# A 64-byte spacer at the right end of SBUF in a one-core decoder-layer kernel

## Chip, core and metric

The kernel runs on one core of one Trainium2 chip. The metric is the device time of one execution in microseconds (us). The core has five engines with queues of their own: TensorE (PE, matmuls, with its weight loads listed as PEld), VectorE (DVE), ScalarE (ACT), GpSimd (POOL) and SyncE (SP, which here only starts DMAs). The on-chip memory SBUF has 128 partitions; a tile takes the same range of bytes in each partition, and "begins at byte b" below means that range.

## The reference

One layer of a hybrid decoder, batch 1, 1024 tokens, width 1024, all in float32:

```
hn = rmsnorm(x);  proj = hn @ w_in          # 3592 columns
attention: 4 heads, two softmaxes each, ALiBi, out = (p0 - lam * p1) @ v
mLSTM:     4 heads, causal conv + silu on q and k, chunked matrix memory
x  = x + concat(da_out, ml_out) @ w_out
hn = rmsnorm(x)
u  = causal_dwconv(hn @ w_up, width 3)      # 2 x 2816 columns
x  = x + (silu(gate) * up) @ w_down
out = rmsnorm(x)
```

## The kernel before

Every large float32 product is made of three PE matmuls on operands that were split into a high and a low part (`split`, L109: ACT writes the high part, DVE or POOL the rest; both lie in one tile `[P, 2, 512]`). `mm3` (L154) issues them as L155, L156 and L157: high times high, high times low, low times high; `mm3b` (L159, lines L160 to L162) does the same in another order. In the rows of the profile the operand behind `<-` that is named first is the **moving** one, which is streamed through the array in 512 columns, and the second the **stationary** one, which is loaded beforehand: `mm<-xb,w` streams `xb` against weights from `w`. Where both come from tiles of one name, the row has the name once (`big<-w`).

The program goes through these stages on the one PE:

1. Input projection and gates (0 to about 215 us): `xb` (the split input) and `w` (split weights), moving and stationary in either role. The gate columns `wg16` (L408) are a small stationary operand of their own.
2. mLSTM chunks (to about 300 us) with the last projections as filler.
3. Attention (to about 500 us), with projections of the next head and of the output as filler; scores are L746 (`ks` against `qs`) and L747 (`kl` against `qz`).
4. Output projection (to about 571 us): stationary `mxT` (L792), moving `w` and then `th`.
5. Up-projection (about 571 to 1004 us): `product` (L1010) runs 154 times, 7 for each of 22 column blocks (a Strassen scheme of 7 products on halves), and issues 12 `mm3` matmuls each time, 1848 in all. Stationary is `w`, written by `prep` (L971), which is kept LEAD = 5 products ahead; moving are the blocks of the activations in `hb`, `th`, `raw`, `B22h`, `B22l` and, for the low parts of some, `x2a`.
6. Down-projection (about 1004 to 1211 us): `dmm` with both operands in tiles `w`, `w2` and the like, then the final norm.

All instructions of an engine stand in the order in which the code issues them; waits follow from the tiles that instructions share. Tiles get their addresses from pools, which are stacks. A pool without a side grows from low bytes upward (`cp`, `sp`, `wp`, `px`, later `px2`, `pmx`, `pf`, `pd`). A pool with `side="right"` grows downward from the top (`pr0`, `pq`, `pa` at L166 to L168; `pb`, `pat`, and for stages 5 and 6 `ph0` and `phn`, which hold `hb`, `B22`, `raw` and `th`). Nearly all tiles have sizes that are multiples of 128 bytes, so all tiles of one side share their start modulo 128, apart from a few small ones and `vext` and `Cst` of the mLSTM.

Of the kernel before, what the change touches and what calls it, by code (L numbers as in the profile page):

```python
# [10 lines left out]
F32 = mybir.dt.float32  # L11
# [6 lines left out]
P = 128  # L18
# [21 lines left out]
def tile_hybrid(ctx: ExitStack, tc: tile.TileContext, I: dict, out: bass.AP):  # L40
# [10 lines left out]
    class Scope:  # L51
# [8 lines left out]

        def close(self):
            self.st.close()

    wp = Scope("wp")

# [1289 lines left out]
```

## Time and profile before

| what | us |
|---|---|
| three runs | 1217.51, 1219.83, 1223.55 (median 1219.83) |
| the profiled execution, whole time | 1226.28 |
| its span, first to last instruction | 1224.5 |
| PE busy in the span | 1196.4 (98%) |
| DVE, ACT, POOL busy | 898.4, 572.5, 476.9 |
| mean granted TensorE clock | 0.995 of full speed |

The page gives busy times of each engine, a strip of 40 slices of the span, the DMA queues, the chain of work that ended last (followed back from the last instruction) and groups of instructions by line with their mean duration. Windows count each engine's busy time and instructions in a stretch of the span; the timeline lists instructions by start. The page says of itself that matmuls are pipelined and that their ends are modelled: a matmul's listed duration overlaps the next one, so the pace of PE is read from starts, or from the number of matmuls in a window in which PE never idles.

### The profile page before, as it was taken

To read this page: it belongs to the slowest core of one execution; us is meant where nothing else is said; L and a number is where in the kernel's file an instruction comes from. 1 tells how busy PE (TensorE), PEld (TensorE's weight loads), DVE (VectorE), ACT (ScalarE), POOL (GpSimd) and SP (SyncE) were. 2 spreads that over 40 slices of the span, in tenths; PEclk is the share of its full clock that TensorE was granted. 3 is DMA by queue.
4 is the path that set the end of the run, shared out by engine and by line. 5 is a ranking of instruction groups with operands and counts; after the bars stand their busy time and mean duration, and the time that the engine had idled before them with its cause. 6 is when DMAs were issued, how large, how long until landed. Compare 5 with 4: busy or idle time off the path is not lost.

```text
span 1224.5 us, 15939 instructions
## 1 busy us (share of the span) xinstructions
PE 1196.4 (98%) x5622; PEld 976.5 (80%) x5622; DVE 898.4 (73%) x1564; ACT 572.5 (47%) x1114; POOL 476.9 (39%) x364
## 2 busy tenths in 40 slices
PE   9998999999999999999999999999999999999996
PEld 7885778888778878888888888888888888888885
DVE  5599222566767777679998978787787778896694
ACT  6533323334666664444643443434344345544462
POOL 0475451004544421001398877777777600000000
PEclk9998999999999999999999999999999999999999
DMA  8755574124222252433222221212212158832223
GB/s 301 260 209 201 212 251 154 62 80 154 80 50 56 65 178 87 144 119 113 85 71 102 90 100 69 86 69 86 88 68 103 53 212 321 307 105 95 95 78 137
DMA packets 61743, 159.03 MB, mean 130 GB/s; under 512 B 6176, under 2 KB 10464, under 8 KB 61664
## 3 DMA queue, kind: packets, MB, share of 16 engines
q1 hardware_dynamic: 61232, 157.21, 37.4%
q8 instruction: 44, 0.72, 0.2%
q10 hardware_dynamic: 432, 0.82, 0.2%
q14 instruction: 35, 0.29, 0.1%
HBM read 116.02 MB, written 37.78 MB: 126 GB/s over the span
## 4 chain that ended last, share of the span: by engine, by line
PE 82%; DVE 6%; DMA 5%; ACT 3%; POOL 3%; issue 1%; SPq 0%; POOLq 0%; DVEq 0%; ACTq 0%
PE mm L157 6%; PE mm L155 6%; PE mm L156 6%; PE big L155 5%; PE big L157 5%; PE big L156 5%; PE mm L160 4%; PE mm L161 4%; PE mm L162 4%; PE big L160 3%; PE big L161 3%; PE big L162 3%; PE sb L774 3%; PE sb L155 2%; PE sa L155 2%; PE sa L157 2%
## 5 line engine op out<-in xcount | busy, mean ns | idle before, releaser
L112 ACT ACTIVATE w<-wf 128x512 fp32r<-128x512 f32 x160 | 98.1, 625 | 139.1 <-PE mm L157 36.6
L113 DVE TENSOR_TENSOR w<-wf,w 128x512 fp32r<-128x512 f32 x128 | 106.1, 840 | 25.8 <-ACT w L112 21.6
L1038 DVE SCALAR_TENSOR_TENSOR y<-x2b,fcw,y 128x1022 f32<-128x1022 f32 x44 | 90.7, 2100 | 0.0
L1037 DVE SCALAR_TENSOR_TENSOR y<-x2b,fcw,y 128x1023 f32<-128x1023 f32 x44 | 75.1, 1745 | 10.6 <-ACT y L1036 10.6
L324 POOL TENSOR_TENSOR vda<-vda 128x512 f32<-128x512 f32 x24 | 47.9, 2011 | 62.1 <-DMA vda<-in_w_down_dram 61.3
L113 POOL TENSOR_TENSOR w<-s,w 128x512 fp32r<-128x512 f32 x40 | 68.8, 1721 | 7.1 <-ACT w L112 7.1
L113 POOL TENSOR_TENSOR w<-wf,w 128x512 fp32r<-128x512 f32 x32 | 46.2, 1446 | 58.0 <-ACT w L112 48.1
L113 POOL TENSOR_TENSOR w<-wu,w 128x512 fp32r<-128x512 f32 x40 | 66.1, 1651 | 4.0 <-ACT w L112 4.0
L155 PE MATMUL mm<-xb,w 128*128 128x512 f32 x168 | 66.2, 394 | 0.0
L157 PE MATMUL mm<-xb,w 128*128 128x512 f32 x168 | 65.9, 392 | 0.0
L156 PE MATMUL mm<-xb,w 128*128 128x512 f32 x168 | 65.9, 392 | 0.0
L749 DVE CUSTOM_DVE_ANT_0 s<-big,B 128x128 f32<-128x128 f32 (+7 forms) x64 | 47.6, 755 | 13.7 <-PE big L747 12.3
L1036 ACT ACTIVATE y<-x2b,fcw 128x1024 f32<-128x1024 f32 x44 | 52.3, 1237 | 11.1 <-DVE x2b L1027 9.7
L965 POOL TENSOR_TENSOR s<-wu 128x512 f32<-128x512 f32 x20 | 32.0, 1601 | 58.5 <-DMA wu<-in_w_up_dram 58.5
L751 ACT ACTIVATE s<-s,mb 128x128 f32<-128x128 f32 (+7 forms) x64 | 49.3, 772 | 11.2 <-DVE mb L750 10.1
L160 PE MATMUL big<-w 128*128 128x512 f32 x132 | 51.5, 390 | 0.8 <-DVE x L1199 0.8
L112 ACT ACTIVATE w<-s 128x512 fp32r<-128x512 f32 x43 | 27.0, 629 | 52.3 <-PE mm L157 18.6
L161 PE MATMUL big<-w 128*128 128x512 f32 x132 | 51.4, 389 | 0.0
L162 PE MATMUL big<-w 128*128 128x512 f32 x132 | 51.4, 389 | 0.0
L112 ACT ACTIVATE w<-wu 128x512 fp32r<-128x512 f32 x48 | 29.7, 626 | 43.7 <-PE mm L157 13.5
L1027 DVE TENSOR_TENSOR x2b<-x2b,mm 128x512 f32<-128x512 f32 x51 | 34.1, 681 | 20.4 <-PE mm L157 19.7
L1027 DVE TENSOR_TENSOR x2b<-x2b,big 128x512 f32<-128x512 f32 x53 | 35.4, 680 | 18.5 <-PE big L157 17.9
(514 smaller groups left out, 3802.5 us busy)
## 6 DMA issues: line engine op xcount, KB each, us to landing
wf<-in_w_up_dram SPq DMA_DIRECT2D x22, 512.0 KB, 4.4
actd<-y SPq DMA_DIRECT2D x21, 512.0 KB, 2.6
wu<-in_w_up_dram SPq DMA_DIRECT2D x20, 512.0 KB, 3.4
wf<-in_w_st_dram SPq DMA_DIRECT2D x12, 512.0 KB, 4.2
vda<-in_w_down_dram SPq DMA_DIRECT2D x12, 512.0 KB, 5.9
wsum<-vda SPq DMA_DIRECT2D x12, 512.0 KB, 3.1
wf<-in_w_mv_dram SPq DMA_DIRECT2D x12, 512.0 KB, 5.2
wf<-wsum SPq DMA_DIRECT2D x12, 512.0 KB, 3.4
```

Source lines behind the costliest of these rows:

```text
L112: A.activation(dst[:, 0, :], src, AF.Copy)
L113: loeng.tensor_tensor(dst[:, 1, :], src, dst[:, 0, :].bitcast(F32), op=ALU.subtract)
L155: PE.matmul(ps, sh, mh, start=first, stop=False)
L156: PE.matmul(ps, sh, ml, start=False, stop=False)
L157: PE.matmul(ps, sl, mh, start=False, stop=last)
L160: PE.matmul(ps, sh, w[:, 0, :], start=first, stop=False)
L161: PE.matmul(ps, sl, w[:, 0, :], start=False, stop=False)
L162: PE.matmul(ps, sh, w[:, 1, :], start=False, stop=last)
L1027: V.tensor_tensor(dst, src, ps, op=ALU.add)
L1036: A.activation(y, u, AF.Identity, bias=cw[:, 3:4], scale=cw[:, 2:3])
L1037: V.scalar_tensor_tensor(y[:, 1:], u[:, :S - 1], cw[:, 1:2], y[:, 1:], op0=ALU.mult, op1=ALU.add)
L1038: V.scalar_tensor_tensor(y[:, 2:], u[:, :S - 2], cw[:, 0:1], y[:, 2:], op0=ALU.mult, op1=ALU.add)
```

## The change

A pool of one tile of 16 float32 (64 bytes in each partition) is opened first on the right side. It is never written or read. Every later pool on the right side starts 64 bytes lower; nothing else in the code differs.

```diff
         def close(self):
             self.st.close()
+
+
+    ctx.enter_context(tc.tile_pool(name="pad", bufs=1, side="right")).tile([P, 16], F32, name="padr")

     wp = Scope("wp")
```

No instruction is added, removed or moved on any engine, and every wait is on the same semaphore and value. What differs is the start byte of 316 of the program's tiles, all on the right side. The two programs place the operands that PE reads most as follows (start byte modulo 128, and where the tiles of that name lie before):

| tile | side | bytes before | before, mod 128 | after, mod 128 |
|---|---|---|---|---|
| `w`, `xb`, `mxT`, `w2`, `x2a` | left | 32416 to 122528 | 32 | 32 |
| `th`, `raw` | right | 126944 to 180192 | 96 | 32 |
| `hb`, `B22h`, `B22l` | right | 180192 to 229344 | 96 | 32 |
| `ks`, `kl`, `qs`, `qz`, `s`, `aT`, `vda`, `mqk`, `ta` | right | 131040 to 221152 | 96 | 32 |
| `wg16` | right | 149728 | 96 | 32 |
| `vext` (two buffers) | right | 135072, 139200 | 32 and 64 | 96 and 0 |
| `Cst` | right | 130944 | 0 | 64 |
| `ident` and the other constants in `cst` | left | 16512 | 0 | 0 |

Slices of these operands start at multiples of 512 bytes in their tiles, except in `wg16` (64), `vext` and `Cst` (516).

## The prediction

> **What bounds the kernel.** First the page's busy times, its strip of the granted clock, and the chain that ended last:
>
> ```profile
> PE 1196.4 (98%) x5622; PEld 976.5 (80%) x5622; DVE 898.4 (73%) x1564; ACT 572.5 (47%) x1114; POOL 476.9 (39%) x364
> ...
> PEclk9998999999999999999999999999999999999999
> ...
> PE 82%; DVE 6%; DMA 5%; ACT 3%; POOL 3%; issue 1%; SPq 0%; POOLq 0%; DVEq 0%; ACTq 0%
> ```
>
> PE is busy for 98% of the span at nearly the full clock and carries 82% of the chain. A busy PE is not yet a PE at its best pace, though: the number of matmuls in a window says how fast it goes. Here are windows of PE alone (window, us, busy, number of matmuls, clock, DMA), in each of which PE issues only matmuls of 512 columns and never idles:
>
> ```profile
> 20.00:50.00 30.00, 30.00 (x134) 1.00 0.84 299
> 60.00:90.00 30.00, 30.00 (x134) 1.00 0.60 218
> 700.00:800.00 100.00, 100.00 (x430) 1.00 0.23 79
> 800.00:900.00 100.00, 100.00 (x430) 1.00 0.23 79
> 1100.00:1200.00 100.00, 100.00 (x443) 1.00 0.32 108
> ```
>
> A matmul's listed duration overlaps its neighbours', so a window counts about two too many: 441 in 100 us is 226.8 ns each in the last window, 428 in 100 us is 233.6 ns in the two of the up-projection, and 132 in 30 us is 227.3 ns in the first two. The instruction, the shape and the clock are the same; **the up-projection's pace is some 3% slower**. The groups by shape inside windows tell which operands go with which pace; the first three rows are of the window 590 to 1004 us, the next of 12 to 92 us, the last of 1006 to 1200 us:
>
> ```profile
> L155 PE MATMUL big<-th,w 128*128 128x512 f32 x120 | 47.7, 397 | 0.0
> ...
> L156 PE MATMUL mm<-hb,w 128*128 128x512 f32 x56 | 22.3, 397 | 0.0
> ...
> L156 PE MATMUL mm<-x2a,w 128*128 128x512 f32 x60 | 23.8, 397 | 0.0
> ...
> L156 PE MATMUL big<-xb,w 128*128 128x512 f32 x42 | 16.3, 389 | 0.0
> ...
> L160 PE MATMUL big<-w 128*128 128x512 f32 x122 | 47.5, 389 | 0.0
> ```
>
> The same line L156 with the same kind of stationary operand (`w`) lasts 389 ns against `xb` and 397 ns against `hb`. What differs is where the moving operand lies: `xb` begins at byte 32 modulo 128, `hb` and `th` at 96. The timeline of PE (start, duration) at the change from the up- to the down-projection gives the pace exactly:
>
> ```profile
> 1000.25 0.40 PE L155 MATMUL sa<-th,w 128*128 128x512 f32 x1
> ...
> 1003.05 0.40 PE L155 MATMUL mm<-B22h,w 128*128 128x512 f32 x1
> ...
> 1004.45 0.40 PE L160 MATMUL big<-w 128*128 128x512 f32 x1
> ...
> 1006.53 0.39 PE L160 MATMUL big<-w 128*128 128x512 f32 x1
> ```
>
> Twelve matmuls from 1000.25 to 1003.05 are 233.3 ns each. The first nine that read left tiles only, 1004.45 to 1006.53, still take 231 ns; then the pace is 226.7 ns to the end. It recovers with a lag of some 2 us. Two more places have a right operand. In the output projection it is the moving one (`th`), in the gate columns the stationary one (`wg16`, the mean of sixteen):
>
> ```profile
> 533.13 0.39 PE L161 MATMUL mm<-th,mxT 128*128 128x512 f32 x1
> ...
> 535.88 0.39 PE L161 MATMUL mm<-th,mxT 128*128 128x512 f32 x1
> ...
> 95.91 0.39 PE L157 MATMUL mm<-xb,w 128*128 128x512 f32 x1
> 96.14 3.87 PE L408 MATMUL sb<-xb,wg 128*16 128x512 f32 x16
> ```
>
> The first two rows are twelve matmuls apart: 229.2 ns. The gate group lasts 3.87 us to the end of its last; with 0.39 us for that one, fifteen steps take 3.48 us, 232 ns, and it follows straight upon `xb,w` at 226.7. **Every stretch with an operand at 96 is slower than 226.7 ns, every stretch with both at 32 runs at it.** The size fits too. 512 columns in 226.7 ns are 0.443 ns a column; 64 bytes are 16 float32 columns, 7.1 ns; the loss is 6.6 ns. It looks like a fetch that moves in steps and loses a step of 64 bytes.
>
> [...]
>
> **The change part by part.** No instruction or wait is added, removed or moved, so the sum consists of new durations alone.
>
> *Up-projection.* 1848 matmuls. All moving tiles but `x2a` go from 96 to 32; `w` stays. From about 587 to 1004.45 us the pace is 233.3 ns; I take 226.7, the nearest row with `mm3`, `w` stationary and both at 32 (`xb,w`). 417 us x (1 - 226.7/233.3) = **-11.8 us**. Bounds: nothing, and the same amount the other way (see the rivals). The 48 or so matmuls before 587 and the 192 of `th,mxT` gain 229.2 - 226.7 = 2.5 ns each: **-0.6 us**. The 32 gate matmuls gain 32 x 5 ns = **-0.2 us**.
>
> *Attention.* 96 score matmuls of 512 columns have both operands on the right:
>
> ```profile
> 430.10 0.40 PE L747 MATMUL big<-kl,qz 128*128 128x512 f32 x1
> 430.33 0.40 PE L746 MATMUL big<-ks,qs 128*128 128x512 f32 x1
> 430.56 0.39 PE L747 MATMUL big<-kl,qz 128*128 128x512 f32 x1
> ```
>
> 230 ns by these starts, 3.3 ns over the fast pace: **-0.3 us**. The small float32 matmuls (L774 and the mLSTM's, where `vext` and `Cst` get other phases) have no row with the new phase. Two rows of the chain in order of time, eight matmuls of 128 columns each, the first streaming `mqk` at 96, the second constants at byte 0:
>
> ```profile
> 223.55 0.89 PE sb L608 x8
> ...
> 530.37 0.87 PE big L907 x8
> ```
>
> 20 ns in eight are 2.5 ns each; with some 500 such matmuls I bound them by 1.3 us either way, and take nothing, since nearly all go from 96 to 32 and not to 0.
>
> *Other engines and DMA.* Does DVE, ACT or a transfer care for the start? Groups of one shape and kind, right and left:
>
> ```profile
> L763 DVE SCALAR_TENSOR_TENSOR s<-s,cc 128x1024 f32<-128x1024 f32 x4 | 5.1, 1287 | 0.1
> ...
> L890 DVE SCALAR_TENSOR_TENSOR y<-x2a,rx,fnw 128x1024 f32<-128x1024 f32 x4 | 5.1, 1284 | 0.1
> ...
> L112 ACT ACTIVATE w<-hb 128x512 fp32r<-128x512 f32 x41 | 25.8, 630 | 45.3 <-PE big L162 19.9 <-PE sa L162 19.2 <-PE sa L157 2.2
> ...
> L112 ACT ACTIVATE w<-s 128x512 fp32r<-128x512 f32 x43 | 27.0, 629 | 52.3 <-PE mm L157 18.6 <-PE big L157 16.9 <-PE sb L157 8.2
> ...
> wsum<-ta SPq DMA_DIRECT2D x10, 512.0 KB, 2.9
> ...
> actd<-y SPq DMA_DIRECT2D x21, 512.0 KB, 2.6
> ```
>
> `s` of L763 and `hb` are at 96, `y` and `s` of L112 at 32: within 0.3%. (Stores from `ta` at 96 and from `y` at 32 differ by 0.3 us, in stages with different traffic.) Nothing for these.
>
> *What is late next.* Will the up-projection keep up with a faster PE? The first window of each engine there, and one later (PE, PEld, DVE, ACT, POOL), with the largest wait that touches PE:
>
> ```profile
> 590.00:640.00 50.00, 50.00 (x216) 40.41 (x216) 48.71 (x47) 25.66 (x36) 34.75 (x20) 1.00 0.26 85
> ...
> 700.00:800.00 100.00, 100.00 (x430) 80.92 (x429) 81.45 (x72) 40.80 (x56) 78.74 (x48) 1.00 0.23 79
> ...
> ACT w L112 <- PE mm L157: 55.0, 29, 2.2
> ```
>
> After 700 us DVE has 18% to spare, and ACT, in the wait shown (window 587 to 1004 us), stands idle until PE gives a `w` tile back, so the preparation is ahead. From 590 to 640 us DVE is 97% busy; PE would need 48.6 us instead of 50 and DVE has 48.7 to do. Some of the 1.4 us can be lost there: **+0.5 us**.
>
> *The sum.* -11.8 - 0.6 - 0.2 - 0.3 + 0.5 = -12.4 us. The profiled execution would go from a span of 1224.5 to 1212.1, and from 1226.3 to 1213.9 as a whole. It was 6.5 us above the median of the runs, 1219.8; by the median the forecast is 1207.4.
>
> [...]
>
> **The rivals.**
>
> *It is the place, not the phase.* Every slow operand lies above byte 126,000, every fast one below 123,000, and the trace has no large matmul operand that is high and at 32. If distance or height costs, the pace stays: **1219.8** (1215 to 1224). For it: `x2a` lies low and at 32 and is yet listed with 397 ns. Against it: each such matmul stands between two that read `th`, and the lag of 2 us after 1004 shows that neighbours pass the slow pace on; and the loss of just 64 bytes' worth of columns is what a phase gives and a distance has no reason to.
>
> *Only partly.* If the up-projection falls to the pace of `th,mxT`, 229.2 ns, the gain is 417 x (1 - 229.2/233.3) = 7.3 us: **1212.5**.
>
> *Slower.* If two streams of the same phase from far parts of SBUF collide, `w` at 32 against `hb` at 32 loses another step: 417 us x 6.6/233.3 = +11.8 us, **1231.6**. It decides as soon as equal phases in different halves cost more than unequal ones. For it: the only pair with both operands on the right, `ks,qs`, is no faster than the mixed ones. Against it: `xb,w` and `w,mxT` have equal phases and run at the fast pace.
>
> **How the numbers follow.** Forecast 0.68, partly 0.08, no effect 0.19, slower 0.05. A measurement of this kernel tells about 0.5%, 6.1 us, from no change. Faster by more: 0.68 + 0.08 = 0.76; within: 0.19; slower: 0.05. The forecast's own range is 1203 to 1212 (runs of one kernel spread by 3 us either way, the small matmuls by 1.3). To hold 8 in 10 the whole range takes in the partial case and the near side of no effect: 1203 to 1219.
>
> **What would show it.** Right: windows of 100 us in the up-projection count about 443 matmuls instead of 430, `hb,w` and `th,w` are listed with 389 ns, the gate group lasts 3.8 us or less, and the down-projection begins about 12 us earlier, at an unchanged pace. Wrong: x430 again, at unchanged order; that makes it the place. If the count rises and the time doesn't fall, PE has got new idle time between 590 and 700 us behind DVE.

## The result and the profile after

| | before | after |
|---|---|---|
| median of nine runs, us | 1226.74 | 1214.42 |
| lowest and highest, us | 1217.51, 1230.15 | 1213.14, 1217.04 |
| the profiled execution, us | 1226.28 | 1213.26 |
| its span, us | 1224.5 | 1211.5 |

The ratio is 0.9915, with a 95% interval from 0.9894 to 0.9936: faster. The medians lie 12.3 us apart (0.990 by themselves), the means 10.6 us and the spans of the profiled executions 13.0 us. One execution of the kernel before, taken beside the last experiment, lasted 4223.57 us and is left out of the ratio there. In the changed kernel the lines of the body carry numbers that are 3 higher: L155 to L157 of `mm3` are now L158 to L160, and L160 to L162 of `mm3b` are L163 to L165.

From the page of the kernel after, busy times, granted clock and the chain that ended last:

```profile
PE 1183.0 (98%) x5622; PEld 973.3 (80%) x5622; DVE 899.2 (74%) x1564; ACT 571.0 (47%) x1114; POOL 480.1 (40%) x364
...
PEclk9998999999999999999999999999999999999999
...
PE 84%; DVE 5%; DMA 3%; ACT 3%; POOL 3%; issue 1%; SPq 1%; POOLq 0%; ACTq 0%; DVEq 0%
```

PE lost 13.4 us of busy time (1196.4 to 1183.0) with the same 5622 matmuls at the same clock. The other engines' busy times move by 3.2 us at most, and PE still bounds the kernel. Where PE got faster is in its windows (window, us, busy, number of matmuls, clock, DMA):

```profile
60.00:90.00 30.00, 30.00 (x134) 1.00 0.56 203
700.00:800.00 100.00, 100.00 (x443) 1.00 0.24 85
800.00:900.00 100.00, 100.00 (x443) 1.00 0.27 89
```

In the up-projection x443 stands where x430 stood; the window of the input projection counts x134 as before. The whole of stage 5, from the first matmul of `hb,w` to the first of the down-projection, is the measure used from here on. First the row of before, then that of after:

```profile
571.14:1004.45 433.31, 433.12 (x1865) 1.00 0.27 93
```

```profile
570.20:991.50 421.30, 421.30 (x1865) 1.00 0.28 95
```

The same 1865 matmuls (1848 of `product`, and transposes) take 12.01 us less. Before the stage the two executions differ by 0.94 us, after it by 0.1 (1224.5 - 1004.45 = 220.05; 1211.5 - 991.50 = 220.0). So **the time came out of the up-projection and nowhere else that can be told**. The groups by shape from 576 to 991 us list the new durations:

```profile
L158 PE MATMUL big<-th,w 128*128 128x512 f32 x120 | 46.7, 389 | 0.0
...
L159 PE MATMUL mm<-x2a,w 128*128 128x512 f32 x60 | 23.3, 389 | 0.0
L159 PE MATMUL big<-x2a,w 128*128 128x512 f32 x56 | 21.8, 389 | 0.0
...
L159 PE MATMUL sb<-x2a,w 128*128 128x512 f32 x36 | 14.0, 389 | 0.0
...
L159 PE MATMUL sa<-x2a,w 128*128 128x512 f32 x24 | 9.3, 389 | 0.0
```

389 ns for all, where `th` and `x2a` had 397; `x2a` too, whose address didn't change. The timeline of PE at the end of the stage (start, duration):

```profile
988.78 0.39 PE L158 MATMUL mm<-B22h,w 128*128 128x512 f32 x1
...
991.50 0.39 PE L163 MATMUL big<-w 128*128 128x512 f32 x1
...
992.18 0.39 PE L163 MATMUL big<-w 128*128 128x512 f32 x1
```

Twelve matmuls from 988.78 to 991.50 are 226.7 ns each, three from 991.50 to 992.18 the same: the lag after the change of stages is gone with the slow pace.

### The profile page after: what moved, and what is told of

The parts are those of the page before. It is cut to its first block, busy times and chain, and to the rows that moved or that the text cites. A ratio compares the mean times of both kernels' runs of the same rounds, so it can differ in the third digit from the quotient of the medians.

```text
span 1211.5 us, 15939 instructions
## 1 busy us (share of the span) xinstructions
PE 1183.0 (98%) x5622; PEld 973.3 (80%) x5622; DVE 899.2 (74%) x1564; ACT 571.0 (47%) x1114; POOL 480.1 (40%) x364
## 4 chain that ended last, share of the span: by engine, by line
PE 84%; DVE 5%; DMA 3%; ACT 3%; POOL 3%; issue 1%; SPq 1%; POOLq 0%; ACTq 0%; DVEq 0%
PE mm L160 6%; PE mm L158 6%; PE mm L159 6%; PE mm L163 5%; PE mm L164 5%; PE mm L165 5%; PE big L158 4%; PE big L160 4%; PE big L159 4%; PE big L164 4%; PE big L165 4%; PE big L163 4%; PE sb L777 3%; POOL vda L327 3%; PE sb L158 2%; PE sb L160 2%
## 5 line engine op out<-in xcount | busy, mean ns | idle before, releaser
L158 PE MATMUL mm<-xb,w 128*128 128x512 f32 x168 | 66.1, 394 | 0.0
L160 PE MATMUL mm<-xb,w 128*128 128x512 f32 x168 | 65.9, 392 | 0.0
L159 PE MATMUL mm<-xb,w 128*128 128x512 f32 x168 | 65.9, 392 | 0.0
L968 POOL TENSOR_TENSOR s<-wu 128x512 f32<-128x512 f32 x20 | 36.5, 1825 | 58.0 <-DMA wu<-in_w_up_dram 58.0
L752 DVE CUSTOM_DVE_ANT_0 s<-big,B 128x128 f32<-128x128 f32 (+7 forms) x64 | 47.6, 755 | 13.7 <-PE big L750 12.3
L1039 ACT ACTIVATE y<-x2b,fcw 128x1024 f32<-128x1024 f32 x44 | 52.3, 1237 | 9.6 <-DVE x2b L1030 8.4
L163 PE MATMUL big<-w 128*128 128x512 f32 x132 | 51.5, 390 | 0.8 <-DVE x L1202 0.8
L165 PE MATMUL big<-w 128*128 128x512 f32 x132 | 51.3, 389 | 0.0
L777 PEld LDWEIGHTS sb<-vda,aT 128*128 128x128 f32 x288 | 36.2, 190 | 15.4 <-ACT aT L774 14.6
L777 PE MATMUL sb<-vda,aT 128*128 128x128 f32 x288 | 44.2, 289 | 3.7 <-ACT aT L774 3.1
L115 ACT ACTIVATE w<-hb 128x512 fp32r<-128x512 f32 x41 | 25.8, 630 | 44.9 <-PE big L165 19.8
```

Of the source, the lines that this page charges most:

```text
L115: A.activation(dst[:, 0, :], src, AF.Copy)
L158: PE.matmul(ps, sh, mh, start=first, stop=False)
L159: PE.matmul(ps, sh, ml, start=False, stop=False)
L160: PE.matmul(ps, sl, mh, start=False, stop=last)
L163: PE.matmul(ps, sh, w[:, 0, :], start=first, stop=False)
L165: PE.matmul(ps, sh, w[:, 1, :], start=False, stop=last)
```

## The experiments

An operand's phase is its start byte modulo some power of two. It is told modulo 256 here; the table in the section on the change has the start bytes modulo 128, which turns out to be too coarse. Left is `w`, `xb`, `mxT`, `x2a`; right is `th`, `hb`, `raw`, `B22h`, `B22l`. Before, left is 160 and right 224; after, both are 160.

### Six spacers: place, phase or difference

All six start from the kernel before. The first three change the right side alone, as the change does, by other amounts.

A spacer of 128 bytes:

```diff
+    ctx.enter_context(tc.tile_pool(name="pad", bufs=1, side="right")).tile([P, 32], F32, name="padr")
```

> Spacer of 128 instead of 64 bytes: right tiles at 96 modulo 128 again (96 instead of 224 modulo 256), left ones at 32. Theory A (the pace of a matmul depends on the phase of each operand modulo 128, 96 being slow) and theory B (only on whether the two operands have the same phase modulo 128): 233 ns a matmul in the up-projection, about 430 matmuls in 100 us, a span 12 us above that of the change. Theory C (what counts is the phase modulo 256, or that the tiles moved at all): 226.7 ns, 443 in 100 us.

A spacer of 96 bytes:

```diff
+    ctx.enter_context(tc.tile_pool(name="pad", bufs=1, side="right")).tile([P, 24], F32, name="padr")
```

> Spacer of 96 bytes: right tiles at 0 modulo 128, left ones at 32. Theory A, with a fetch that starts better the more of its first 128 bytes it uses: the up-projection at or below 226.7 ns, 443 or more matmuls in 100 us. Theory B (unequal phases are slow): above 226.7 ns, some 430 to 437 in 100 us.

A spacer of 192 bytes:

```diff
+    ctx.enter_context(tc.tile_pool(name="pad", bufs=1, side="right")).tile([P, 48], F32, name="padr")
```

> Spacer of 192 bytes on the right: right tiles at 32, left ones at 160 modulo 256, so equal modulo 128 (both 32) and unequal modulo 256. B modulo 128: the up-projection at 226.7 ns, 443 in 100 us, the span of the change. B modulo 256: slow, 230 to 233 ns, 430 to 435 in 100 us, a span 8 to 12 us above that of the change.

The other three move the left side, ahead of all large left tiles. 64 bytes on the left alone:

```diff
-    wp = Scope("wp")
+    ctx.enter_context(tc.tile_pool(name="padl", bufs=1)).tile([P, 16], F32, name="padl"); wp = Scope("wp")
```

> No spacer on the right, one of 64 bytes on the left ahead of the first large pool: left and right tiles both at 96 modulo 128. Theory A: all stages slow, 233 ns also in the input and down-projection, 430 matmuls in 100 us there, a span some 12 us or more above that of before. Theory B: all stages fast, 226.7 ns, a span as with the change.

96 bytes on either side:

```diff
+    ctx.enter_context(tc.tile_pool(name="pad", bufs=1, side="right")).tile([P, 24], F32, name="padr")
-    wp = Scope("wp")
+    ctx.enter_context(tc.tile_pool(name="padl", bufs=1)).tile([P, 24], F32, name="padl"); wp = Scope("wp")
```

> Spacers of 96 bytes on both sides: all large tiles at 0 modulo 128. Theory B: 226.7 ns everywhere, a span as with the change. Theory A with a fetch of 128 bytes: faster still, by up to the 8 columns that a start at 32 leaves out of its first 128 bytes (3.3 ns of 226.7, 1.5%), 223.3 ns, 449 matmuls in 100 us in all stages, a span some 14 us below that of the change.

32 bytes on either side:

```diff
+    ctx.enter_context(tc.tile_pool(name="pad", bufs=1, side="right")).tile([P, 8], F32, name="padr")
-    wp = Scope("wp")
+    ctx.enter_context(tc.tile_pool(name="padl", bufs=1)).tile([P, 8], F32, name="padl"); wp = Scope("wp")
```

> Spacers of 32 bytes on both sides: all large tiles at 192 modulo 256. After the first four runs theory B stands: a matmul is slow when its moving and its stationary operand differ in phase, modulo 256 rather than 128. B: 226.7 ns in all stages, 443 matmuls in 100 us, the span of the change. Theory A in what is left of it (the phase as such counts besides, a multiple of 64 being better than 32): below 226.7 ns, more than 443.

Each had one execution; the kernel before took 1227.94 us on the same chip. Stage 5 in the windows of PE, one kernel after another in the order of the table below:

```profile
572.70:1006.14 433.44, 433.34 (x1866) 1.00 0.27 93
```

```profile
573.81:1006.92 433.11, 433.03 (x1865) 1.00 0.27 93
```

```profile
573.10:1002.73 429.63, 429.61 (x1865) 1.00 0.27 93
```

```profile
576.53:1006.01 429.48, 429.48 (x1866) 1.00 0.27 93
```

```profile
572.35:993.88 421.53, 421.41 (x1865) 1.00 0.28 95
```

```profile
572.72:994.07 421.35, 421.35 (x1865) 1.00 0.28 95
```

| spacers, bytes | left, right mod 256 | right less left | stage 5, us | whole time, us |
|---|---|---|---|---|
| none (before) | 160, 224 | 64 | 433.31 | 1226.28 |
| 64 right (the change) | 160, 160 | 0 | 421.30 | 1213.26 |
| 128 right | 160, 96 | -64 | 433.44 | 1227.91 |
| 96 right | 160, 128 | -32 | 433.11 | 1228.69 |
| 192 right | 160, 32 | -128 | 429.63 | 1224.55 |
| 96 left, 96 right | 0, 128 | 128 | 429.48 | 1227.76 |
| 64 left | 224, 224 | 0 | 421.53 | 1215.66 |
| 32 left, 32 right | 192, 192 | 0 | 421.35 | 1215.85 |

Only the column of differences orders the times. **Stage 5 takes 421.3 to 421.5 us when both sides have the same phase, at 160, 192 or 224, and 429.5 to 433.4 us when they haven't.** The absolute phase, which the prediction took for the cause, falls on two rows: with all tiles at 96 modulo 128 (64 left) the stage is fast, and with the right side at 0 modulo 128 (96 right) it is as slow as before. The place falls with 128 right: the same tiles within 64 bytes of where the change has them, and no gain. Equal phases modulo 128 don't do either: 192 right has both sides at 32 modulo 128, and gains only 3.7 us of the 12. And 512 isn't needed: after the change `w` begins at 32416 and `th` at 147360, which is 160 and 416 modulo 512, and the stage takes 421.30 us. So 256 is the period, for these tiles.

The whole times order less well (1227.76 against 1224.55 for one and the same stage length), since the stages before differ too, in part between executions of one kernel: the first `hb,w` comes between 570.20 and 576.53 us in these rows.

### Is it the pairing of operands? One side taken apart into two phases

With the change in place, a pad ahead of one left pool puts only some of the left tiles at 224. First `xb`, the operand of the input projection:

```diff
-    px = Scope("px")
+    px = Scope("px"); px.t([P, 16], tag="padx")
```

> The change, with a second spacer of 64 bytes at the start of the pool px: of the large operands xb alone goes to 224 modulo 256, against 160 for w and everything on the right. B: the input projection (20 to 90 us) slows down from 226.7 to 229 to 233 ns, 130 to 132 matmuls in 30 us instead of 134; the up-projection stays at 443 in 100 us; with 1344 matmuls that read xb the span rises by 3 us (at 229 ns) to 9 us (at 233). Any theory in which the right side or the height of the tiles matters: no change of the input projection.

Windows of the input projection and of the up-projection:

```profile
20.00:50.00 30.00, 30.00 (x131) 1.00 0.83 294
60.00:90.00 30.00, 30.00 (x133) 1.00 0.57 205
700.00:800.00 100.00, 100.00 (x442) 1.00 0.25 85
```

x131 against the x135 and x134 of the change and of before in the first window, and 1217.38 us as a whole. A stretch that had been fast in both kernels has become slow, with both operands on the left side, while the up-projection stays fast. So it isn't a property of the up-projection or of the right side.

The second window counts x133, more than the 130 to 132 expected. The timeline has two slow paces for the same tiles, the same difference and the same lines of code:

```profile
31.30 0.40 PE L158 MATMUL mm<-xb,w 128*128 128x512 f32 x1
...
34.10 0.40 PE L158 MATMUL mm<-xb,w 128*128 128x512 f32 x1
...
76.41 0.39 PE L159 MATMUL mm<-xb,w 128*128 128x512 f32 x1
...
79.16 0.39 PE L159 MATMUL mm<-xb,w 128*128 128x512 f32 x1
```

Twelve matmuls are 233.3 ns each in the first pair of rows and 229.2 ns each in the second. Between them, from 52.3 to 53.6 us, stand eight small matmuls of other operands. The kernel before has the same two paces for `hb,w`: twelve from 581.93 us are 229.2 ns each and twelve from 632.29 us 233.3. So at a difference of 64 the operands' phases alone don't fix the pace; that what came before has a part in it is a guess, and no run shows what sets it.

Then `x2a` and `mxT`, by the same pad in the pool `px2`, again on top of the change:

```diff
-                px2 = Scope("px2")
+                px2 = Scope("px2"); px2.t([P, 16], tag="padx")
```

> The change, with a second spacer of 64 bytes at the start of the pool px2: x2a (and mxT) go to 224 modulo 256, w, th, hb and raw stay at 160. In the up-projection only the middle one of the triples th, x2a, th has unequal phases, 176 of 1848 matmuls. B matmul by matmul: these triples last 687 ns instead of 680, 442 in 100 us, +1.2 us there. B with a carry-over to the neighbours, as x2a seemed to suffer before: the triples last up to 700 ns, about 439 in 100 us, up to +3.5 us. Besides, the 384 matmuls with mxT slow down by 2 to 7 ns each, 1 to 2.5 us, in both.

The timeline of PE where a product that reads `x2a` ends:

```profile
702.64 0.40 PE L158 MATMUL big<-th,w 128*128 128x512 f32 x1
702.87 0.40 PE L159 MATMUL big<-x2a,w 128*128 128x512 f32 x1
703.10 0.39 PE L160 MATMUL big<-th,w 128*128 128x512 f32 x1
703.34 0.40 PE L158 MATMUL big<-th,w 128*128 128x512 f32 x1
703.57 0.39 PE L159 MATMUL big<-raw,w 128*128 128x512 f32 x1
...
704.26 0.39 PE L159 MATMUL big<-raw,w 128*128 128x512 f32 x1
...
706.98 0.39 PE L159 MATMUL sb<-raw,w 128*128 128x512 f32 x1
```

Only the middle one of each three with `x2a` is unequal, yet the three from 702.64 to 703.34 take 0.70 us, against 0.68 for three at 226.7. The three from 703.57 to 704.26, all with equal phases again, still take 0.69; the twelve from 704.26 to 706.98 take 2.72, the fast pace. **Here an unequal matmul slows the equal ones that follow it, and the pace comes back about five matmuls after the last unequal one** (the five from 703.10 to 704.26 are 232 ns each, the next twelve 226.7). The bill of the stage agrees:

```profile
573.64:997.86 424.22, 424.22 (x1866) 1.00 0.28 95
```

424.22 less 421.30 is 2.92 us, and the groups of after count 60 + 56 + 36 + 24 = 176 threes with `x2a`: 16.6 ns for each, where one matmul alone at the old pace would cost 6.6. As a whole the kernel took 1219.63 us; from the first matmul with `mxT` to stage 5 it needs 1.7 us more than after the change, within the 1 to 2.5 us expected for that. The bill also clears up `x2a` in the profile before, listed with 397 ns although its phase was that of `w`: it stood between two unequal matmuls.

### Own operands, or the load beside them

The trace lists the load of the next matmul's stationary operand within the time of the matmul before: below, the load for L159 starts at 705.23 us together with the matmul of L158 and is listed with 0.19 us, and the matmul of L159 starts at 705.45. The timeline of the kernel after, matmuls and weight loads (PEld):

```profile
705.23 0.39 PE L158 MATMUL mm<-B22h,w 128*128 128x512 f32 x1
705.23 0.19 PEld L159 LDWEIGHTS mm<-B22l,w 128*128 128x128 f32 x1
705.45 0.39 PE L159 MATMUL mm<-B22l,w 128*128 128x512 f32 x1
705.46 0.19 PEld L160 LDWEIGHTS mm<-B22h,w 128*128 128x128 f32 x1
```

So the phases that must agree could be those of a matmul's own two operands, or of the moving one and the load beside it. In the runs so far all stationary operands of a stretch had one phase, so they can't tell. Two kernels on top of the change give the low half of `w` a phase of its own. The first:

```diff
     def wtile():
-        return wp.t([P, 2, 512], F32R, "w", 8)
+        return wp.t([P, 1088], F32R, "w", 8)[:, 0:1056].rearrange("p (a b) -> p a b", a=2)[:, :, 0:512]
...
-        f = wp.t([P, 1024], F32, "wf", 2)
+        f = wp.t([P, 1024], F32, "wf", 1)
```

(and one buffer of `wf` at its other three places). The letters A and B mean in these two expectations what they say there.

> The change, and in every w tile the low half begins 64 bytes later than before (at 224 modulo 256, the high half stays at 160); wf has one buffer instead of two to make room, which may cost some time of its own. A product in the up-projection goes: high moving on w high, low moving on w high, high moving on w low. Each matmul's stationary operand is loaded while the matmul ahead of it streams. Theory A (what must agree is a matmul's own two operands): the third matmul of each three is unequal, and with the neighbours it touches the whole up-projection goes at 229 to 233 ns, x429 to x437 in 100 us. Theory B (what must agree is the moving operand and the stationary one that is loaded beside it, that is the next matmul's): the second of each three is unequal, and the result is the same 229 to 233 ns. Both: all stages with w slower than 226.7 ns, the down-projection too (x385 to x396 in 1100 to 1190 us). This run is the control for the next.

The second adds the pad in `px2`:

```diff
-                px2 = Scope("px2")
+                px2 = Scope("px2"); px2.t([P, 16], tag="padx")
```

> As the run before, and x2a (the low moving operand of some of the threes) also at 224, as in the run with the pad in px2. Theory A (own operands): in the threes with x2a two of three matmuls are unequal; they go at 229 to 233 ns like the rest, x429 to x437 in 100 us, no stretch at 226.7. Theory B (moving operand and the load beside it): in these threes each stream has a load of its own phase beside it: high (160) beside w high (160), low (224) beside w low (224), high (160) beside the next w high (160). In the stretch of 24 matmuls with x2a that follow each other in the products T2, T3 and T1, all but about the first five to nine go at 226.7 ns, while the threes with raw, B22l and hb stay at 229 to 233. The run with the pad in px2 alone had these very threes as the only slow ones of the up-projection, so the two theories differ in sign here.

Windows of the first, then its groups by shape from 590 to 1020 us (the three are issued as L158, L159, L160; the rows stand by cost):

```profile
700.00:800.00 100.00, 100.00 (x435) 1.00 0.24 83
800.00:900.00 100.00, 100.00 (x434) 1.00 0.23 79
...
1100.00:1190.00 90.00, 90.00 (x393) 1.00 0.30 100
```

```profile
L160 PE MATMUL big<-hb,w 128*128 128x512 f32 x64 | 25.4, 397 | 0.0
...
L159 PE MATMUL big<-hb,w 128*128 128x512 f32 x64 | 25.1, 392 | 0.0
L158 PE MATMUL big<-hb,w 128*128 128x512 f32 x64 | 25.0, 390 | 0.0
```

All stages with `w` are slower, the down-projection too (x393 in 90 us, where before and after have x399). The longest of the three is the third, the one whose own stationary operand is off. The decision is in the second kernel, in its timeline within the run of 24 matmuls with `x2a`:

```profile
725.05 0.40 PE L158 MATMUL mm<-th,w 128*128 128x512 f32 x1
...
727.13 0.40 PE L158 MATMUL mm<-th,w 128*128 128x512 f32 x1
...
728.52 0.40 PE L158 MATMUL big<-th,w 128*128 128x512 f32 x1
```

Nine matmuls from 725.05 to 727.13 are 231.1 ns each, and the six to 728.52 are 231.7. Had the load beside the stream been what must agree, these would have been the fast ones, at 226.7. **So the load beside the stream is ruled out.** That a matmul's own moving and stationary operand must agree fits all runs; that any operands read near each other in time must agree would make these threes slow too, and no run parts those two. The whole times of the two, 1257.38 and 1258.97 us, hold the single buffer of `wf` as well: the first `hb,w` comes 21.6 and 23.0 us later than after the change, and they are not compared.

### The equal phase from the other side, timed

The kernel with 64 bytes on the left once more, with enough runs for an interval.

> The kernel before with 64 bytes on the left instead of the right, all large tiles at 224 modulo 256, now timed. Relative phase alone counts: 12 us faster than before, a ratio of 0.990 to 0.991, the same as the change has. If the absolute phase gives or takes a part that a single look hid, the ratio differs from the change's 0.9915 by more than 0.002.

Its median was 1214.17 us against 1227.01 for the kernel before, a ratio of 0.9896 (0.9874 to 0.9918); stage 5 in its windows:

```profile
571.03:992.54 421.51, 421.39 (x1865) 1.00 0.28 95
```

The interval takes in most of the change's own (0.9894 to 0.9936), and the stage is 0.2 us from that of the change. The ratios are 0.0019 apart, barely inside the 0.002 that the expectation allowed. So moving the left side up instead of the right side down is worth the same as far as these runs tell, and neither place nor absolute phase adds anything that can be told from them. No version was found that beats the change. All tiles at 0 modulo 256 would need a total of 320 bytes, and between the highest `xb`, which ends at byte 130720, and `Cst` at 130944 the kernel before leaves 224: that wasn't tried.

## Why the prediction was right, and where it wasn't

**What bounds the kernel** held: PE, whose pace differed by operands (233.3 and 226.7 ns) at one shape and one clock.

**The up-projection.** Predicted -11.8 us from `th` on, and 0.1 for the 48 or so matmuls ahead of it; stage 5 gave -12.0. The count of x443, the 389 ns and the down-projection at an unchanged pace came as stated. The size was read from a row with the right property (equal phases), so it held although the reason given for it didn't. That is luck: the spacer that takes the right side away from 96 also happens to give it the phase of the left. Asked about 64 bytes on the left, the prediction's reason would have forecast a slower kernel, and that one took 1215.66 us.

**The reason failed.** "Every stretch with an operand at 96 is slower, every stretch with both at 32 runs at it" was true of the rows of before, but there the phase and the difference go together in all large products: left was always at 32, and right always at 96. The step from "these two differ" to "the one at 96 is the slow one" had no row behind it, and the spacers of 96 bytes on the right (433.11 us in stage 5) and 64 on the left (421.53) part the two. The reading of the 6.6 ns as a fetch that loses a step of 64 bytes falls in the same way: with every large tile at 96 modulo 128 stage 5 takes 421.53 us, and nothing is lost.

**The rivals.** The place was wrong, and its one argument, the slow `x2a`, was the carry-over. It could have been doubted from the kernel before: the table of addresses leaves out that one `xb` lies from 126624 to 130720, in bytes that `raw` takes later, and all of `xb,w` from 60 to 90 us ran at 226.7 ns. So "every fast one below 123,000" was wrong. "Slower" was wrong in its sign: it is equal phases that are fast. Its argument was that `ks,qs` with both operands on the right is no faster. That pair had equal phases before and after, so **the term of -0.3 us for the attention had no ground**. It comes at most four in a row, between blocks of small matmuls, and there another equal pair is as slow. After the change, directly behind such a block and one `kl,qz`:

```profile
432.68 0.40 PE L158 MATMUL mm<-xb,w 128*128 128x512 f32 x1
...
433.84 0.40 PE L160 MATMUL mm<-xb,w 128*128 128x512 f32 x1
```

These first five `xb,w` are 232 ns each, where the later ones go at 226.7. The phases of the small matmuls aren't the reason: with 96 right, `ks`, `qs` and the `cst` and `s` of the small ones ahead of them are all at 128 modulo 256, and `ks,qs` still takes some 235 ns (432.10 to 432.57 us, two matmuls). Why equal pairs start slow behind a block of small matmuls is not shown. "Partly" (229.2 ns) is the lesser of the two slow paces that a difference of 64 has.

**The gate columns.** Predicted -0.2 us and 3.8 us or less for the group; the timeline of after has

```profile
96.09 3.88 PE L411 MATMUL sb<-xb,wg 128*16 128x512 f32 x16
```

3.88 us, against 3.87 before. The slices of `wg16` are 64 bytes apart, so at any start only one in four can agree with `xb`; the section on the change said so below its table, and the prediction passed over it.

**The DVE-bound window.** Predicted +0.5 us between 590 and 640 us:

```profile
590.00:640.00 50.00, 50.00 (x222) 41.13 (x221) 49.10 (x46) 25.07 (x35) 35.91 (x20) 1.00 0.24 82
```

DVE is busy for 49.10 of the 50 us, and PE still counts 220 in 50 us (two taken off, as in the prediction), 227.3 ns each: 220 x 0.6 ns is 0.1 us. The preparation was far enough ahead.

**The output projection.** Predicted -0.5 us for the 192 of `th,mxT`. Their pace came as stated (twelve from 532.51 to 535.23 us are 226.7 ns each), but from the first of them to the first `hb,w` it is 52.31 us against 52.48, only 0.17 less. Each group of 24 stands behind small matmuls, and its first twelve go at 227.5 to 231 ns after the change too.

**The 0.9 us before stage 5** can't be credited to `th,mxT`, gate and scores. The first `ks,qs` of the attention stands 0.7 us earlier already, and executions of one kernel vary as much: with 64 bytes on the left the first `hb,w` came at 572.35 us in one and at 571.03 in another.

**The level.** The sum of -12.4 us stands against -12.3 between medians, -10.6 between means and -13.0 between the profiled executions. The measured 1214.42 lies above the forecast's own range of 1203 to 1212; the stated 1203 to 1219 holds it only because it was widened for the rivals of a partial effect and of none. The partial rival's 1212.5 is the nearer number, and by the time alone the two could not be told apart; the pace of 226.7 ns in stage 5 decides for the forecast. The 1207.4 was 7 us low because it was counted from the median of three runs that all lay below the six that came later (1217.51 to 1223.55 against 1225.20 to 1230.15). Counted from the profiled execution, 1213.9 was forecast and 1213.26 measured; that was the better base.

## What to carry to other kernels

Where large matmuls run back to back and PE is the bound, compare the pace by operand pair (the number of matmuls in windows without idle time or small matmuls). If, as in this kernel, one pair is 1 to 3% slower at one shape and clock, compare the start bytes of its moving and stationary tiles modulo 256, the period found here. A spacer at the start of one side's pools (64 bytes here) brings them to one phase without an instruction more (5622 matmuls before and after), and either side can be the one that moves (1214.42 us with the right, 1214.17 with the left, against about 1227). Before blaming a property of one operand, ask whether the rows could tell it from the relation of the two; a run that gives both the suspected value does.

## What the runs showed of the hardware

- The pace of float32 matmuls of 512 columns, with a weight load each, depends on the start bytes of the moving and the stationary operand modulo 256: 226.7 ns when equal (x442 or x443 in 100 us of the up-projection, with both at 160, 192 or 224), some 231.5 ns at a difference of 128 or -128 (x434), some 233.3 at +64, -64 and -32 (x430; at +64 in some stretches 229.2). What in the chip does this isn't known from these runs.
- The phases of the two operands don't tell the whole pace. At a difference of 64 one pair of tiles in one kernel goes at 233.3 ns in one stretch and 229.2 in another (`xb,w` with the pad in `px`, `hb,w` before). With one unequal matmul in three all three are slow (0.70 us for three, against 0.68), and it takes about five equal ones (some nine at the end of stage 5 before) to get back to 226.7. Behind a block of small matmuls, equal pairs too start slowly: five `xb,w` at 232 ns, the first twelve of each group of `th,mxT` at 227.5 to 231.
- Where only the low half of `w` is 64 bytes off, which the third matmul of each three reads, that costs two thirds of the full loss: x434 to x435 in 100 us, between x443 and x430.
